# Two heads' attention scores of the prompt as one product with 128 stationary columns

## The chip, the cores and the metric

The kernel runs on one core of a Trainium2 chip. Its engines work from queues of their own: TensorE (PE in the rows, with its weight loads as PEld), VectorE (DVE), ScalarE (ACT), GpSimd (POOL) and SyncE (SP, which here issues the transfers). The metric is the device time of one launch in microseconds (us), as the median of the runs; lower is better. Before the change it is 1457.76 us.

## The reference

Two layers of a streaming encoder run over 512 prompt frames and 8 running streams of 16 frames, model width 1024. Each layer does

    hn   = rms_norm(x);  proj = hn @ w_in            # u_a, g_a, u_b, q, k, v
    out_a = RG-LRU(u_a, g_a)                          # conv, gates, linear scan
    out_b = S5(u_b)                                   # complex state space scan
    out_c = attention(rope(q), rope(k), v)            # 8 query heads, 2 kv heads, 64 wide
    x = x + concat(out_a, out_b, out_c) @ w_out
    x = x + square(relu(rms_norm(x) @ w_up)) @ w_down

and a last norm follows. The change is in the prompt's attention. Frames are in chunks of 64; a chunk's queries see their own chunk's keys and those of the two chunks before (64 keys for the first chunk, 128 for the second, 192 from then on). Four query heads share one kv head, and a learned sink enters each softmax:

    scores = einsum('bnqkgd,bnskd->bnkgqs', qc, kb) * 64 ** -0.5
    probs  = sink_softmax(scores, sinks, mask)
    out    = einsum('bnkgqs,bnskd->bnqkgd', probs, vb)

## The kernel before

All frames are in two groups g of 320 columns: 256 prompt frames and 64 frames of four streams. Activations stand with the features on the 128 partitions. A weight product (`product`, lines L252 to L254) makes a tile of 128 by 320 from 24 matmuls: the weights are split into a high part `wh` (ScalarE, L243) and a low part `wl` (VectorE, L244), each made for four of the eight blocks of 128 rows at a time. So every 12 matmuls need one `wh` and one `wl`, and a late `wl` holds TensorE up in the row L254.

The program writes, for a layer, the input projection of a group (`in_proj`), then the group's mixers (`lru`, `s5`, `attention`), and then output projections and MLP. The order on each engine is not the written one: a list scheduler with a time model of its own places every instruction when the program is built, so products fill TensorE while the mixers' short steps go through VectorE, ScalarE and GpSimd. Whatever changes an instruction's modelled time can move all that follow. Each engine then runs its queue strictly in the order placed.

`attention` works through chunks cq = 0 to 3 and both kv heads. `probs` (L869 to L879) makes the scores of four heads in a PSUM bank: two pairs pr of two heads s each, on the partitions 64 s to 64 s + 63. Query head tile i = 2 pr + s holds kv head 0 on the partitions 0 to 63 and kv head 1 on 64 to 127, so one matmul (L878) contracts over 64 partitions, has 64 stationary columns (a chunk's queries of one head) and streams nk = 64, 128 or 192 keys. In fp32 each written matmul is two records in the trace; per call of `probs` there are 8, and 32 calls in the program. Then `soft` takes the maximum (L818), the offset (L822), the exponentials (ACT, L824) with sums, and scales (L828 to L833). `turned` (transposes L176, copies L890 and L892) and `values` (L899, outputs L903 and L904) follow. Scores, transposes and values share the two PSUM banks `att`. The streams' own attention has its scores in L839, copies in L849 and its values in L857.

Other names that matter: S5's output matmuls L753 and L755, which wait for VectorE's L744; S5's input products L721, which contract over 64 partitions with 128 stationary columns; L269 splits the normalised activations of the next product, L689 and L783 the mixers' outputs; L739 and L680 are scans; L663 the RG-LRU gate products. The rotated queries are written by L609 in `in_evac`.

Of the kernel before, what the change touches and what calls it, by code (L numbers as in the profile page):

```python
# [11 lines left out]
F32 = mybir.dt.float32  # L12
# [38 lines left out]
def _cols(a):  # L51
    """(..., 128 r) vectors as columns."""
    a = np.asarray(a)
    return a.reshape(-1, 128).T
# [5 lines left out]
def _layout(inputs):  # L60
    """The arrays in the order in which the chip reads them: moves of elements only."""
# [6 lines left out]
    def tiles(w):  # L68
        # (1024, 128 n) -> (n, 128 p, 8 k, 128)
        return w.reshape(8, 128, -1, 128).transpose(2, 1, 0, 3)  # L70
# [9 lines left out]
    # small vectors, one column each  # L80
# [13 lines left out]
    # S5 input and output matrices: halves (re, im) and (im, re) on the partitions  # L94
# [53 lines left out]
def encoder_kernel(ctx: ExitStack, tc: tile.TileContext, a, o):  # L148
# [35 lines left out]
    # ------------------------------------------------------------ constants  # L184
# [4 lines left out]
    # the table of the exponentials comes in before the first load has landed  # L189
# [41 lines left out]
    # ------------------------------------------------------------ weights  # L231
# [25 lines left out]
    # ------------------------------------------------------------ norms  # L257
    class Norm:
# [41 lines left out]
        def rsqrt(self):  # L300
            """8/3 / sqrt(mean + eps) with the tokens on the partitions (0-127, 128-255, 192-319)."""
            x = self.bank[:, 320:323]
            w = tp.tile([128, 2, 3], F32, tag="rsq", name="rsq", bufs=2)
            wi = tp.tile([128, 3], I32, tag="rsqi", name="rsqi", bufs=2)
            t, y = (w[:, i] for i in range(2))
            y0 = wi.bitcast(F32)
            # a first guess from the exponent, one step of second order and one of third
            V.tensor_scalar(wi, x.bitcast(I32), -0.5, 1597463007.0, OP.mult, OP.add)
            V.scalar_tensor_tensor(t, y0, -0.5, y0, OP.mult, OP.mult)
            tt(t, t, x, OP.mult)  # L310
            V.scalar_tensor_tensor(y, t, 1.5, y0, OP.add, OP.mult)
            V.scalar_tensor_tensor(t, y, -1.0, y, OP.mult, OP.mult)
            tt(t, t, x, OP.mult)
            V.scalar_tensor_tensor(y0, t, 10.0 / 3, t, OP.add, OP.mult)
            V.scalar_tensor_tensor(y, y0, 5.0, y, OP.add, OP.mult)
            return y
# [14 lines left out]
    # ------------------------------------------------------------ small vectors  # L331
# [6 lines left out]
    # ------------------------------------------------------------ accurate exp on small tiles  # L338
    def exp_small(out, x, n):
        """out = exp(x) on [128, n], to about one unit in the last place."""  # L340
        w = stile(128, 4, n)
        k, f, p, e = (w[:, i] for i in range(4))
        ki = stile(128, n).bitcast(I32)
        V.tensor_scalar(k, x, 1.4426950408889634, 12582912.0, OP.mult, OP.add)
        V.tensor_scalar(k, k, 12582912.0, None, OP.subtract)
        V.tensor_scalar(k, k, -126.0, 126.0, OP.max, OP.min)
        V.scalar_tensor_tensor(f, k, -0.693359375, x, OP.mult, OP.add)
        V.scalar_tensor_tensor(f, k, 2.12194440054690583e-4, f, OP.mult, OP.add)
        V.tensor_scalar(p, f, 1.0 / 5040, 1.0 / 720, OP.mult, OP.add)
        for c in (1.0 / 120, 1.0 / 24, 1.0 / 6, 0.5, 1.0, 1.0):  # L350
            tt(p, p, f, OP.mult)
            V.tensor_scalar(p, p, c, None, OP.add)
        V.tensor_scalar(e, k, 127.0, 8388608.0, OP.add, OP.mult)
        V.tensor_copy(ki, e)
        tt(out, p, ki.bitcast(F32), OP.mult)

    # ------------------------------------------------------------ LRU constants
# [24 lines left out]
    # ------------------------------------------------------------ S5 constants  # L382
# [49 lines left out]
    def cmul(eng, out, jout, wr, wis, z, jz, tmp, conj=False):  # L432
        """out = w z (stacked halves), jout = its halves swapped; wis has the half's sign."""
# [9 lines left out]
    def s5_const(L):  # L443
# [10 lines left out]
        # input matrices: slot s of a pair of groups is abar^(3-s) Bbar  # L454
# [15 lines left out]
        # output matrices  # L470
# [9 lines left out]
        # causal products inside a block: those with the block's last output, then the rows moved up  # L480
# [9 lines left out]
        # rotation tables by doubling  # L490
# [37 lines left out]
    # ------------------------------------------------------------ per layer small tensors  # L528
# [12 lines left out]
    # ------------------------------------------------------------ input projection  # L541
    def gelu2(eng, out, x):
        """out = 2 gelu(x)"""
        w = tp.tile([128, NG], F32, tag="gw", name="gw", bufs=1)
        eng.tensor_tensor(w, x, x, OP.mult)
        eng.tensor_scalar(w, w, 0.044715, 1.0, OP.mult, OP.add)
        eng.tensor_tensor(w, w, x, OP.mult)
        act(w, w, AF.Tanh, scale=0.7978845608028654)
        V.scalar_tensor_tensor(out, w, 1.0, x, OP.add, OP.mult)
# [4 lines left out]
    def in_alloc():  # L554
# [3 lines left out]
        q.q = tp.tile([128, 4, 256], F32, tag="q", name="q", bufs=2)  # L558
# [6 lines left out]
    def in_evac(L, P, g, q, kind, i, pt):  # L565
# [34 lines left out]
        else:  # L600
# [5 lines left out]
            if kind == "q":  # L606
                t = tp.tile([128, NG], F32, tag="t", name="t", bufs=2)
                tt(t, pt, q.cosr, OP.mult)
                tt(q.q[:, i], t[:, 0:256], sw[:, 0:256], OP.add)  # L609
# [31 lines left out]
    # ------------------------------------------------------------ RG-LRU  # L641
    def lru(L, P, g, q, mix, c):
# [10 lines left out]
        for ct in range(2):  # L653
# [4 lines left out]
            # the newest rows before the convolution  # L658
# [7 lines left out]
            # decay a = exp(-2 w) and 1 - a^2 = tanh(w) (1 + a)^2  # L666
# [7 lines left out]
        # injection of the running states into the column before each sample  # L674
# [18 lines left out]
    # ------------------------------------------------------------ S5  # L693
    def s5(L, P, g, q, mix, c):
        K = P["S5"]
        u = q.ub
        # zz takes the place of U
# [5 lines left out]
        # inputs by blocks: rows (group of the pair, t, channel)  # L703
# [41 lines left out]
        # outputs  # L745
# [18 lines left out]
        # states after the last block  # L764
# [22 lines left out]
    # ------------------------------------------------------------ attention  # L787
    def attention(L, P, g, q, mix, c):
        # the samples' scratch
        kcT, p = c.at(0, 2, 2, 144), [c.at(640 + 288 * n, 2, 144) for n in range(2)]  # L790
        vc, pt = c.at(1280, 2, 2, 128), [c.at(640 + 288 * n, 2, 128) for n in range(2)]
        # those of the second pair of samples start at partition 32
        half = [slice(32 * n, 32 * n + 16) for n in range(2)]
        vn, pn = ([c.at(o, 2, 128)[h] for h in half] for o in (1792, 2048))
        # the prompt's, in the same place: keys' windows of 192 columns with 64 zeros on each side
# [18 lines left out]
        def soft(b, x, sk, nsk, one):  # L814
            """Exponentials of the scores in b over their sum with the sink's."""
# [53 lines left out]
        def probs(cq, kv):  # L869
            j, kts, nk, k0, st, w0 = geo(cq)  # L870
            pe, ps, q0 = pes[kv], slice(64 * kv, 64 * kv + 64), 64 * cq
# [4 lines left out]
            for pr in range(2):  # L876
                for s in range(2):
                    mm(b[64 * s:64 * s + 64, pr, 0:nk], lhsT=q.q[ps, 2 * pr + s, q0:q0 + 64], rhs=kT[ps, k0:k0 + nk], start=True, stop=True)  # L878
# [53 lines left out]
    # ------------------------------------------------------------ output projection and MLP  # L932
# [39 lines left out]
    # ------------------------------------------------------------ the program  # L972
# [14 lines left out]
    # the tensor engine's clock rises while the first loads are under way  # L987
# [31 lines left out]
    # ------------------------------------------------------------ final norm  # L1019
# [36 lines left out]
```

## Time and profile before

| | |
|---|---|
| median of 3 runs | 1457.76 us (1455.7 to 1457.97) |
| the profiled execution (its span, first to last instruction) | 1454.2 us |
| what the median has beside the span | 3.6 us |
| TensorE busy | 1404.7 us, 97% |
| VectorE busy | 924.5 us, 64% |
| ScalarE, GpSimd busy | 662.4 us, 377.0 us |
| mean granted TensorE clock | 0.979 |

Time lost shows in three ways: as idle time of the engine that sets the pace, as busy time that a different shape would shorten, and as stretches in which the granted TensorE clock is 0.50. The profile's busy time of TensorE counts pipelined matmuls with modelled ends, so how long a block of matmuls takes is read from its start to the start of what follows.

### The profile page before, as it was taken

The numbers are of one execution on the slowest core, as the hardware profiler recorded it, in microseconds if no ns is written. First come the engines' busy times: TensorE is split into PE (matmuls) and PEld (weight loads), VectorE is DVE, ScalarE is ACT, GpSimd is POOL, SyncE is SP. The second block draws the span as 40 slices with busy tenths as digits, with TensorE's granted clock in tenths as the row PEclk, the third lists the DMA queues.
The fourth block names the chain that finished last, engine by engine and source line by source line (L and its number), as shares of the span: only waits on it lengthen the run. The fifth ranks groups of instructions, "written<-read, shape, count | busy, mean of one in ns | idle before, by whom it ended". The sixth has DMA issues, their size and how long they took to land.

```text
span 1454.2 us, 25829 instructions
## 1 busy us (share of the span) xinstructions
PE 1404.7 (97%) x9540; PEld 1336.3 (92%) x9540; DVE 924.5 (64%) x1858; ACT 662.4 (46%) x1387; POOL 377.0 (26%) x565
## 2 busy tenths in 40 slices
PE   7699999999999999999999999999999999999997
PEld 7688688899999999999987898789999999999997
DVE  8999889856544344357687768875664434434564
ACT  6566565545422122135674667453543312313543
POOL 3847269401010011072244225320110100100111
PEclk9999899999999999999998999899999999999998
DMA  6232122344422222234422342224443222223452
GB/s 244 86 109 81 50 95 97 105 150 140 152 80 78 76 80 73 73 107 157 140 91 73 120 137 92 68 95 145 149 146 106 73 73 73 80 78 104 153 174 94
DMA packets 91389, 156.27 MB, mean 107 GB/s; under 512 B 14336, under 2 KB 18304, under 8 KB 91264
## 3 DMA queue, kind: packets, MB, share of 16 engines
q1 hardware_dynamic: 91264, 154.63, 32.0%
q8 instruction: 75, 1.23, 0.4%
q14 instruction: 50, 0.41, 0.1%
HBM read 151.02 MB, written 3.37 MB: 106 GB/s over the span
## 4 chain that ended last, share of the span: by engine, by line
PE 80%; DVE 11%; POOL 4%; issue 3%; ACT 2%; DMA 1%; SPq 0%; DVEq 0%; POOLq 0%
PE mm L254 24%; PE mm L252 24%; PE mm L253 24%; DVE wl L244 2%; PE att L899 1%; PE att L878 1%; PE s L755 1%; PE s L753 1%; PE att L176 1%; PE s L176 1%; PE fin L326 0%; PE att L663 0%; PE s L721 0%; PE s L779 0%; DVE bigr L269 0%
## 5 line engine op out<-in xcount | busy, mean ns | idle before, releaser
L254 PE MATMUL mm<-bigr,wl 128*128 128x320 f32 x2688 | 840.9, 314 | 22.6 <-DVE wl L244 22.6
L252 PE MATMUL mm<-bigr,wh 128*128 128x320 f32 x2688 | 840.2, 313 | 1.7 <-ACT wh L243 1.1
L253 PE MATMUL mm<-bigr,wh 128*128 128x320 f32 x2688 | 839.1, 313 | 1.0 <-DVE bigr L269 1.0
L243 ACT ACTIVATE wh<-raw 128x512 fp32r<-128x512 f32 x544 | 340.7, 630 | 494.4 <-PE mm L253 469.9
L254 PEld LDWEIGHTS mm<-bigr,wl 128*128 128x128 f32 x2688 | 509.8, 190 | 34.7 <-DVE wl L244 27.4
L252 PEld LDWEIGHTS mm<-bigr,wh 128*128 128x128 f32 x2688 | 509.4, 190 | 7.9 <-issue 5.0
L253 PEld LDWEIGHTS mm<-bigr,wh 128*128 128x128 f32 x2688 | 509.5, 190 | 6.9 <-issue 3.9
L244 DVE TENSOR_TENSOR wl<-raw,wh 128x512 fp32r<-128x512 f32 x544 | 399.7, 736 | 179.6 <-ACT wh L243 158.9
L156 POOL TENSOR_SCALAR bigr<-t 128x320 fp32r<-128x320 f32 x128 | 63.0, 493 | 566.3 <-ACT t L952 566.3
L934 DVE TENSOR_TENSOR xT<-xT,mm 128x320 f32<-128x320 f32 x160 | 77.7, 486 | 127.5 <-PE mm L254 127.4
L952 ACT ACTIVATE t<-t 128x320 f32<-128x320 f32 x128 | 59.9, 470 | 137.9 <-DVE t L951 132.3
L954 DVE TENSOR_TENSOR bigr<-t,bigr 128x320 fp32r<-128x320 f32 x128 | 69.7, 546 | 69.6 <-POOL bigr L156 69.3
L951 DVE SCALAR_TENSOR_TENSOR t<-mm,r 128x320 f32<-128x320 f32 x124 | 60.6, 488 | 81.5 <-PE mm L254 81.4
L288 POOL TENSOR_TENSOR ss<-ss,sq 128x320 f32<-128x320 f32 x58 | 56.9, 981 | 195.7 <-ACT sq L281 185.6
L833 POOL TENSOR_SCALAR att<-att,st 128x192 f32<-128x192 f32 (+3 forms) x40 | 37.2, 931 | 79.5 <-DVE st L831 43.6
L824 ACT ACTIVATE att<-att,st 128x192 f32<-128x192 f32 (+3 forms) x80 | 30.7, 389 | 28.3 <-DVE st L822 22.1
L269 DVE SCALAR_TENSOR_TENSOR bigr<-xT,sm,bigr 128x320 fp32r<-128x320 f32 x64 | 39.7, 629 | 3.8 <-ACT bigr L268 3.6
L268 ACT ACTIVATE bigr<-xT,sm 128x320 fp32r<-128x320 f32 x64 | 34.4, 558 | 11.1 <-DVE xT L934 7.8
L281 ACT ACTIVATE sq<-xT 128x320 f32<-128x320 f32 x66 | 30.4, 460 | 9.9 <-DVE xT L934 3.7
L878 PE MATMUL att<-kT,q 64*64 64x192 f32 (+2 forms) x256 | 28.1, 329 | 2.5 <-ACT att L824 2.1
L605 POOL TENSOR_TENSOR sw<-sw,cs 128x320 f32<-128x320 f32 x20 | 19.4, 969 | 33.6 <-ACT sw L604 28.3
L176 PE MATMUL att<-ident,att 128*128 128x128 f32 (+1 forms) x144 | 24.6, 280 | 3.2 <-DVE att L833 1.0
(287 smaller groups left out, 1078.6 us busy)
## 6 DMA issues: line engine op xcount, KB each, us to landing
raw<-w_up SPq DMA_DIRECT2D x192, 256.0 KB, 2.6
raw<-w_down SPq DMA_DIRECT2D x192, 256.0 KB, 2.6
raw<-w_in SPq DMA_DIRECT2D x96, 256.0 KB, 2.6
raw<-w_out SPq DMA_DIRECT2D x64, 256.0 KB, 2.5
xT<-x SPq DMA_DIRECT2D x8, 320.0 KB, 5.7
yT<-xT SPq DMA_DIRECT2D x8, 320.0 KB, 2.5
cs<-rope SPq DMA_DIRECT2D x4, 320.0 KB, 4.4
gg<-gg SPq DMA_DIRECT2D x2, 512.0 KB, 5.1
```

Of the source, the lines that this page charges most:

```text
L156: return G.tensor_scalar(out, in_, 1.0, 0.0, OP.mult, OP.add)
L176: PE.transpose(out, in_, ident[0:n, 0:n])
L243: act(h, raw, AF.Copy)
L244: tt(l, raw, h.bitcast(F32), OP.subtract)
L252: mm(pt, lhsT=h[:, k % 4], rhs=m[:, k, 0], start=k == 0, stop=False)
L253: mm(pt, lhsT=h[:, k % 4], rhs=m[:, k, 1], start=False, stop=False)
L254: mm(pt, lhsT=l[:, k % 4], rhs=m[:, k, 0], start=False, stop=k == 7)
L288: G.tensor_tensor(self.ss, self.ss, sq, OP.add)
L934: tt(xT[:, g, k], xT[:, g, k], pt, OP.add)
L951: V.scalar_tensor_tensor(t, pt, 0.0, norm.r, OP.max, OP.mult)
L952: act(t, t, AF.Square)
L954: tt(am[:, f, 1], t, am[:, f, 0].bitcast(F32), OP.subtract)
```

## The change

The queries' tile gets the order head pair partition, chunk, head, query (`[128, 4, 4, 64]`, as the streams' tile `qS` has it), so that a chunk's queries of two heads lie in one run of 128 columns. L609 writes it with four runs of 64 elements. `probs` makes a pair's scores in one matmul with 128 stationary columns, in place of two with 64 columns each on the two halves of the PSUM partitions. Operands, key columns, sums and the PSUM tile are otherwise the same. The diff without removed comments:

```
-        q.q = tp.tile([128, 4, 256], F32, tag="q", name="q", bufs=2)
+        q.q = tp.tile([128, 4, 4, 64], F32, tag="q", name="q", bufs=2)
...
-                tt(q.q[:, i], t[:, 0:256], sw[:, 0:256], OP.add)
+                c4 = lambda z: z[:, 0:256].rearrange("p (c q) -> p c q", q=64)
+                tt(q.q[:, :, i], c4(t), c4(sw), OP.add)
...
-            pe, ps, q0 = pes[kv], slice(64 * kv, 64 * kv + 64), 64 * cq
+            pe, ps = pes[kv], slice(64 * kv, 64 * kv + 64)
...
             for pr in range(2):
-                for s in range(2):
-                    mm(b[64 * s:64 * s + 64, pr, 0:nk], lhsT=q.q[ps, 2 * pr + s, q0:q0 + 64], rhs=kT[ps, k0:k0 + nk], start=True, stop=True)
+                mm(b[:, pr, 0:nk], lhsT=q.q[ps, cq, 2 * pr:2 * pr + 2].rearrange("p i q -> p (i q)"), rhs=kT[ps, k0:k0 + nk], start=True, stop=True)
```

The lines from L609 to L877 of the kernel before are one further down in the one after, and L878 stays L878. The scheduler places the instructions anew. Up to the first L878 the order is the same; it differs from there to about 300 us of the trace before, and in small moves in the second layer between 750 and 970 us. Two places follow.

TensorE's queue in the first layer, group 0, ahead of S5's first output matmuls (L755 before, L756 after). Before:

```order
L252 MATMUL mm<-bigr,wh 128x320
L755 MATMUL s_1154<-Cm,bigf 80x64
...
L755 MATMUL s_1155<-Cm,bigf 80x64
L878 MATMUL att<-kT,q 64x192 x4
L899 MATMUL att<-att,vt 64x256 x2
```

After:

```order
L254 MATMUL mm<-bigr,wl 128x320
L878 MATMUL att<-kT,q 128x192 x2
L899 MATMUL att<-att,vt 64x256 x2
L252 MATMUL mm<-bigr,wh 128x320
...
L756 MATMUL s_1154<-Cm,bigf 80x64
L756 MATMUL s_1155<-Cm,bigf 80x64
```

The scores of a chunk and the values of the chunk before it have moved from behind S5's output matmuls to six product matmuls ahead of them.

VectorE's queue in the first layer, group 1, around two successive low parts `wl` of the output projection's weights. In the kernel before (the two `wl` are the third and the fifth row):

```order
L830 TENSOR_TENSOR st_2300<-st_2300 128x2
L680 SCALAR_TENSOR_TENSOR bigf<-bigf,coll 128x332 x2
L244 TENSOR_TENSOR wl<-raw,wh 128x512
L830 TENSOR_TENSOR st_2315<-st_2315 128x2
L244 TENSOR_TENSOR wl<-raw,wh 128x512
```

In the kernel after (L745, L850, L819 and L690 are L744, L849, L818 and L689 of before; the two `wl` are the second and the last row):

```order
L745 TENSOR_TENSOR bigf<-bigf 128x640
L244 TENSOR_TENSOR wl<-raw,wh 128x512
L850 COPY att<-att 16x256
L819 TENSOR_REDUCE st_2321<-att 128x2
L690 SCALAR_TENSOR_TENSOR bigr<-bigf,bigr 128x2x320
L269 SCALAR_TENSOR_TENSOR bigr<-xT,sm,bigr 128x320 x2
L745 TENSOR_TENSOR bigf<-bigf 128x640
L269 SCALAR_TENSOR_TENSOR bigr<-xT,sm,bigr 128x320
L244 TENSOR_TENSOR wl<-raw,wh 128x512
```

Between the two `wl` stands one short step before, and seven steps, most of them long, after; the scans L680 and the streams' softmax steps have moved ahead of both.

## Rows read from the trace of the kernel before

**Rows 1.** The page: busy time, share of the span and instructions of TensorE.

```profile
PE 1404.7 (97%) x9540; PEld 1336.3 (92%) x9540; DVE 924.5 (64%) x1858; ACT 662.4 (46%) x1387; POOL 377.0 (26%) x565
```

**Rows 2.** Windows: stretch, its length, busy time by engine, granted clock, DMA.

```profile
99.00:152.00 53.00, 47.82 (x334) 42.13 (x332) 52.51 (x124) 33.66 (x88) 36.07 (x44) 0.89 0.28 87
150.85:161.05 10.20, 9.72 (x51) 7.42 (x52) 8.25 (x23) 4.88 (x17) 3.00 (x8) 0.50 0.32 105
161.10:200.00 38.90, 38.57 (x262) 29.61 (x261) 27.87 (x58) 25.43 (x58) 12.01 (x15) 1.00 0.15 50
200.00:220.00 20.00, 16.68 (x108) 15.49 (x106) 20.00 (x27) 10.78 (x27) 16.28 (x17) 0.83 0.30 95
220.00:260.00 40.00, 39.33 (x275) 32.98 (x275) 39.09 (x75) 20.50 (x54) 38.91 (x53) 0.96 0.29 94
1000.00:1400.00 400.00, 400.00 (x2732) 399.62 (x2732) 199.93 (x358) 140.48 (x246) 35.20 (x64) 1.00 0.32 108
```

**Rows 3.** Timeline of TensorE: score blocks of 192, 128, 64 keys, and what follows.

```profile
141.86 0.87 PE L878 MATMUL att<-kT,q 64*64 64x192 f32 x8
142.66 0.41 PE L254 MATMUL mm<-bigr,wl 128*128 128x320 f32 x1
...
119.56 0.65 PE L878 MATMUL att<-kT,q 64*64 64x128 f32 x8
120.15 0.41 PE L254 MATMUL mm<-bigr,wl 128*128 128x320 f32 x1
...
99.23 0.45 PE L878 MATMUL att<-kT,q 64*64 64x64 f32 x8
99.61 0.63 PE L253 MATMUL mm<-bigr,wh 128*128 128x320 f32 x1
```

**Rows 4.** Timeline of TensorE: matmuls with 128 stationary columns, and what follows.

```profile
180.16 0.82 PE L663 MATMUL att<-bigf,gg 128*128 128x332 f32 x2
180.92 1.12 PE L721 MATMUL s<-bigf,Bm 64*128 64x80 f32 x8
181.96 0.41 PE L252 MATMUL mm<-bigr,wh 128*128 128x320 f32 x1
```

**Rows 5.** Groups of VectorE by shape: busy us, mean ns of one.

```profile
L609 DVE TENSOR_TENSOR q<-t,sw 128x256 f32<-128x256 f32 x16 | 7.4, 465 | 0.0
```

**Rows 6.** Timeline of TensorE around S5's first output matmuls.

```profile
151.33 0.80 PE L755 MATMUL s<-Cm,bigf 128*80 128x64 f32 x4 [1.48 <-DVE bigf L744]
...
155.62 1.55 PE L878 MATMUL att<-kT,q 64*64 64x192 f32 x8
157.09 1.12 PE L899 MATMUL att<-att,vt 128*64 128x256 f32 x4
158.14 0.64 PE L253 MATMUL mm<-bigr,wh 128*128 128x320 f32 x1
```

**Rows 7.** Timeline of TensorE: the longest wait of group 1.

```profile
206.55 0.64 PE L254 MATMUL mm<-bigr,wl 128*128 128x320 f32 x1 [2.81 <-DVE wl L244]
```

**Rows 8.** Timeline of VectorE, steps that the change puts between two `wl`.

```profile
214.75 0.68 DVE L244 TENSOR_TENSOR wl<-raw,wh 128x512 fp32r<-128x512 f32 x1
...
215.75 1.69 DVE L744 TENSOR_TENSOR bigf<-bigf 128x640 f32<-128x640 f32 x1
...
224.44 1.49 DVE L689 SCALAR_TENSOR_TENSOR bigr<-bigf,bigr 128x640 fp32r<-128x640 f32 x1
225.86 0.55 DVE L818 TENSOR_REDUCE st<-att 128x2 f32<-128x384 f32 x1
...
227.10 1.10 DVE L269 SCALAR_TENSOR_TENSOR bigr<-xT,sm,bigr 128x320 fp32r<-128x320 f32 x2
...
228.62 0.99 DVE L269 SCALAR_TENSOR_TENSOR bigr<-xT,sm,bigr 128x320 fp32r<-128x320 f32 x1
```

**Rows 9.** Timeline of TensorE: S5's output matmuls of group 1, and what follows.

```profile
212.31 0.44 PE L755 MATMUL s<-Cm,bigf 128*80 128x64 f32 x4
...
214.70 0.39 PE L253 MATMUL mm<-bigr,wh 128*128 128x320 f32 x1
```

## Prediction

> **What bounds the kernel now.** I read the page's first part, then windows, then the timelines of TensorE and VectorE around the score matmuls. TensorE is busy for 97% of the span [rows 1], and from 1000 to 1400 us it is busy all the time: 400 us for 2732 matmuls, 0.146 us for a product matmul [rows 2]. There TensorE's work is the time. In the first layer's mixers it is not so throughout. From 99 to 152 us VectorE is busy for 52.51 of 53.00 us, TensorE for 47.82; from 200 to 220 us VectorE for all 20.00, TensorE for 16.68; from 220 to 260 both nearly always (39.09 and 39.33 of 40) [rows 2]. Between, from 161 to 200 us, TensorE is the one that never rests: 38.57 of 38.90 us. So a TensorE edit counts in full in the MLP and in the stretches between, and little where VectorE sets the pace; there the order of VectorE's queue counts. One more thing costs time: from 150.85 to 161.05 us the granted clock is 0.50, which is 1.2 of 2.4 GHz [rows 2]; what stands ahead of its fall is told with term 2.
>
> **The score matmuls themselves.** The names say that half of the matmuls go. What they cost is read from a block's start to the start of what follows: 0.80 us with 192 keys (141.86 to 142.66), 0.59 with 128 (119.56 to 120.15), 0.38 with 64 (99.23 to 99.61) [rows 3]. Each block has 8 records. From 128 to 192 keys it grows by 0.21 us, 3.3 ns a key; one record takes 0.83 ns a key, as L663 shows: two records of 332 columns in 0.76 us with the fixed parts [rows 4], of which 2 x 332 x 0.83 are 0.55. So the block grows as four records do, not as eight: eight in a row would need 8 x 0.16 = 1.28 us alone, and the block has 0.80. The two heads' matmuls, on the two column halves, already run side by side. The new block has four records of as many keys, in four slots: nothing is won from the halved count.
>
> What it adds is the weight load. 128 stationary columns from 64 partitions are what L721 has: eight records of 80 columns take 1.04 us (180.92 to 181.96) [rows 4]. Streaming would be 8 x 80 x 0.83 ns = 0.53; so the load sets the step. With the last record's streaming (0.07) and the 0.09 that the fixed end takes, 0.88 are left for eight loads, 0.11 each. The block of 192 keys has 0.80 - 4 x 0.16 = 0.16 of fixed parts: the same 0.09 and 0.05 to 0.07 for the first load of 64 columns. So the load takes 0.11 with 128 columns and half of that with 64, and it hides under a record that streams longer. New blocks:
> - 192 keys: 0.11 + 4 x 0.16 + 0.09 = 0.84 to 0.85, against 0.80: 0.05 more, for the first load;
> - 128 keys: 4 x 0.11 + 0.11 + 0.09 = 0.64 against 0.59: 0.05 more;
> - 64 keys: load-bound, 4 x 0.11 + 0.05 + 0.09 = 0.58 against 0.38: 0.20 more.
>
> Of 32 blocks, 24 have 192 keys, 4 have 128 and 4 have 64. Five (two, two and one) lie before 152 us, where VectorE covers them; they cost 0.6 if that cover is gone. The rest are 23 x 0.05 + 2 x 0.05 + 2 x 0.20 = 1.65; one of the short ones of the second layer runs at the lower clock, where it costs twice as much. **Term 1: +1.8 us**; bounds 0 (every first load hidden behind the matmul ahead) and +2.4 (no cover).
>
> The Trainium skill has a rule that goes further against the change: "TensorE: Matmul & The Clock Gate", "Part 3: Packing small matmuls", lets a weight load overlap a running matmul only when their row groups differ. By that rule the new records, all on one row group, would each pay their load. The rows differ: L663's two records use all rows, and 0.76 us hold one load (0.11), 0.55 and 0.09, not two loads. What the rule would give as a mechanism of this kernel is the fourth rival.
>
> **The write of the queries.** L609 takes 465 ns as one run of 256 [rows 5]; it becomes four runs of 64. The 16 of them lie in the input projections beside product matmuls. I take 0; bounds from a tenth less to a tenth more, 16 x 0.05 = 0.7 either way, only if VectorE is last there.
>
> **The moved order, group 0 of the first layer.** Before, TensorE comes to S5's output matmuls at 151.33 after a wait of 1.48 us for L744, and the lower clock sets in there; scores and values of a chunk come after them, 155.62 to 158.14 us, 2.52 us at the lower clock [rows 6]. In the new order these two stand ahead. Their softmax steps have moved up on VectorE too, so I expect them to be ready. They take 0.85 + 1.05 = 1.9 us at the higher clock and so fill the wait. VectorE's L744 itself gets later by what is now ahead of it, a copy of 256 columns (put at the 0.47 of L609's 256 [rows 5]) and two steps of two columns (put at 0.2 each): about 0.9. So 2.52 leave the path and 0.9 come in. **Term 2: -1.6 us**; bounds -2.5 (no delay) and +0.9 (scores not ready, delay in full). In 99 to 152 us the set of VectorE's steps is otherwise the same up to a few places, and it is the bound: 0.
>
> **The moved order, group 1 of the first layer.** Two low parts that follow each other with a step of 0.15 between now have 1.69 (L744), 1.49 (L689), 0.55 (L818), 1.10 and 0.99 (three L269) between them [rows 8], 5.8 us, and the second itself takes 0.7. TensorE has in this time, counted from L744's end: S5's output matmuls, 212.31 to 214.70, 2.4 us [rows 9], transposes 0.4, eleven product matmuls 1.6: 4.4 us. The first low part takes 0.7 of VectorE in front. So the second comes 0.7 + 5.8 + 0.7 = 7.2 us after L744, and TensorE stands for 2.8 us. Against that, the streams' transposes, a score block and the scans have been done ahead, while TensorE waited for `wl` anyway: the trace has 2.81 us of such a wait [rows 7]. I set 1.4 of it against the new wait: half of the old wait filled. **Term 3: +1.4 us**; bounds -2.8 (all of the old wait gone and no new one) and +2.8.
>
> In the second layer the blocks move by a few matmuls, with VectorE's queue nearly as before; SP's queue moves some small transfers by a few places. I take 0 for both.
>
> **The sum.** 1454.2 of the profiled span + 3.6 that the median has beside it = 1457.8; + 1.8 - 1.6 + 1.4 = **1459.4 us**, 0.1% above the median. About 0.2% (2.9 us) is what a measurement of this kernel can tell from no change.
>
> **Rivals.**
> 1. *The clock stays up.* With the wait ahead of S5's output matmuls filled, the stretch 150.85 to 161.05 is granted 2.4 GHz. It then has 5.1 us to give; VectorE is busy in it for 8.25 of 10.20 us, which leaves some 2 to 4. For it: the fall stands right behind the wait. Against: the new order has a short wait there still (0.9 less the fill). With term 3 at 0: 1459.4 - 4 - 1.4 = 1454.0. This is the way to a faster kernel.
> 2. *The new wait of group 1 is paid in full and lowers the clock.* The place is the second `wl` behind L744, L689 and L269. The price is 2.8 for the wait, and as before behind the wait of 2.81, a stretch at the lower clock: 20 us at 0.83 [rows 2] are 3.4 lost. 1457.8 + 1.8 - 1.6 + 2.8 + 3.4 = 1464.2. It decides from the point where TensorE's waits between 203 and 222 us sum to over 5 us, against 3.3 (16.68 busy of 20) before.
> 3. *The change does what its name says:* the heads' matmuls ran one after another, and half goes: 24 blocks x 4 x 0.16 + 4 x 4 x 0.11 + 4 x 4 x 0.05 = 18 us, 1440. The blocks' lengths speak against it.
> 4. *No load overlaps in the new block* (the rule above): three more loads of 0.11 in each of 32 blocks, 10.6 us, 1470. L663 speaks against it.
>
> **How the numbers follow.** Forecast 0.43, its own range 1456 to 1462; rival 1 0.25; rival 2 0.27; rival 3 0.02; rival 4 0.03. The order is most of the uncertainty, since a scheduler that places everything anew can win or lose a wait of 3 us, and the clock doubles what a wait costs. Range 1452 to 1465: it takes in rivals 1 and 2 and leaves out 3 and 4 and the tails. Faster: rivals 1 and 3, 0.27. Slower: rivals 2 and 4, 0.30. Within 0.2%: 0.43.
>
> **What would show it.** L878 with 128 records of form 64*128; a block of 192 keys 0.84 to 0.85 us long up to what follows, of 64 keys near 0.58. If 0.80 stands, term 1 is wrong; if near 0.45, the pairs never overlapped; if over 1.1, loads are paid each. For term 2: L878 and L899 ahead of the first L755, and no wait over 1 us at it. For term 3: a wait of 2 to 3 us at a low-part row L254 after S5's output matmuls of group 1. The forecast as a whole is wrong if the stretch 99 to 300 us changes by over 3 us either way, or if the second layer does.

## The result and the profile after

The changed kernel takes 1464.93 us (median of 4 runs, 1463.28 to 1466.50) against 1457.26 for the kernel before on the same chip: a ratio of 1.0055, with a 95% interval of 1.0041 to 1.0069. On a second chip (below) it was 1.0041, from 1.0024 to 1.0057. So it is slower by 0.4 to 0.55%, 6 to 8 us; the forecast of 1459.4 us, no change, was wrong, although the time lies in the range given.

The page of the kernel after, its first part (answering to [rows 1]) and the group of score matmuls from its fifth part (line, engine, operation, tiles, shape, count | busy us, mean ns of one | idle before):

```profile
PE 1414.7 (97%) x9412; PEld 1347.0 (92%) x9412; DVE 925.5 (63%) x1858; ACT 664.5 (45%) x1387; POOL 380.7 (26%) x565
...
L878 PE MATMUL att<-kT,q 64*128 64x192 f32 (+2 forms) x128 | 28.8, 348 | 0.3 <-ACT att L825 0.2
```

The same group in the kernel before:

```profile
L878 PE MATMUL att<-kT,q 64*64 64x192 f32 (+2 forms) x256 | 28.1, 329 | 2.5 <-ACT att L824 2.1 <-DVE st L830 0.4
```

128 records have gone, as the name of the change says, and TensorE is busy for 10.0 us longer. The score group itself takes no less with half the records: 28.8 us against 28.1. The other engines are busy about as long as before.

Windows of the kernel after (stretch, length, busy time of TensorE, its weight loads, VectorE, ScalarE, GpSimd, granted clock, DMA share, GB/s), the first four answering to rows of [rows 2]:

```profile
99.00:152.00 53.00, 48.04 (x311) 41.85 (x310) 51.06 (x123) 33.28 (x89) 34.29 (x43) 0.93 0.26 81
200.00:220.00 20.00, 17.60 (x124) 15.43 (x123) 20.00 (x28) 11.29 (x24) 17.95 (x14) 1.00 0.29 96
220.00:260.00 40.00, 37.67 (x236) 31.43 (x235) 36.06 (x71) 19.63 (x56) 39.88 (x53) 0.87 0.27 88
1000.00:1400.00 400.00, 400.00 (x2733) 399.81 (x2732) 197.26 (x347) 139.61 (x243) 32.54 (x60) 1.00 0.32 107
...
164.60:174.80 10.20, 9.93 (x36) 6.25 (x35) 6.14 (x20) 3.30 (x14) 1.88 (x2) 0.50 0.00 0
226.00:236.20 10.20, 10.20 (x55) 8.34 (x52) 7.55 (x15) 3.85 (x12) 10.20 (x17) 0.50 0.18 61
```

The MLP is as it was (400 us, 2733 matmuls). The stretch at 0.50 that began behind the wait of 1.48 us [rows 6] has shrunk from 10.20 to 3.4 us, but two new ones of 10.20 us stand at 164.60 and 226.00, where TensorE hardly waits at all: 9.93 and 10.20 us busy. Summed over the span, the two profiles have 60.9 us at 0.50 before and 74.8 after (the 63 and 77 of the expectations below take in some 2 us behind the span's end), while TensorE's waits of over 0.15 us come to 42.4 and 42.5.

TensorE's timeline after (start, length, engine, line, operation, tiles, shape, count, in brackets the wait ahead and what ended it). Blocks of 64, 128 and 192 keys answer to [rows 3], the waits to [rows 6, 7, 9]:

```profile
113.32 0.66 PE L878 MATMUL att<-kT,q 64*128 64x64 f32 x4
113.90 0.42 PE L254 MATMUL mm<-bigr,wl 128*128 128x320 f32 x1
...
122.44 0.71 PE L878 MATMUL att<-kT,q 64*128 64x128 f32 x4
123.08 0.42 PE L254 MATMUL mm<-bigr,wl 128*128 128x320 f32 x1
...
149.49 0.41 PE L254 MATMUL mm<-bigr,wl 128*128 128x320 f32 x1 [2.41 <-DVE wl L244]
149.83 0.92 PE L878 MATMUL att<-kT,q 64*128 64x192 f32 x4
151.21 1.12 PE L899 MATMUL att<-att,vt 128*64 128x256 f32 x4 [0.46 <-DVE att L892]
...
154.02 0.57 PE L756 MATMUL s<-Cm,bigf 128*80 128x64 f32 x4
...
162.17 0.92 PE L878 MATMUL att<-kT,q 64*128 64x192 f32 x4
163.02 0.33 PE L176 MATMUL att<-ident,att 128*128 128x128 f32 x1
...
210.25 0.41 PE L254 MATMUL mm<-bigr,wl 128*128 128x320 f32 x1 [0.58 <-DVE wl L244]
...
215.71 0.50 PE L756 MATMUL s<-Cm,bigf 128*80 128x64 f32 x4 [1.17 <-DVE bigf L745]
...
220.99 0.42 PE L254 MATMUL mm<-bigr,wl 128*128 128x320 f32 x1 [0.57 <-DVE wl L244]
...
773.88 0.41 PE L254 MATMUL mm<-bigr,wl 128*128 128x320 f32 x1 [1.54 <-DVE wl L244]
...
776.58 0.79 PE L756 MATMUL s<-Cm,bigf 128*80 128x64 f32 x4 [1.41 <-DVE bigf L745]
```

In the second layer the kernel before has one wait there, not two:

```profile
769.64 0.50 PE L755 MATMUL s<-Cm,bigf 128*80 128x64 f32 x4 [1.74 <-DVE bigf L744]
```

Where it went, counted by the product matmuls (L252 to L254), which both kernels issue in the same number: the start of the 1250th, near 330 us, is 5.7 us later after than before and stays so until 624 us; the 5000th, near 990 us, is 10.5 us later and stays so to the end. So these two profiles lose 5.7 us in the first layer's mixers, 4.8 around the second's, and nothing elsewhere.

Within the first layer the count of product matmuls alone misleads, because the new order has moved other matmuls past them. At the starts of the 580th, the 640th and the 1040th both kernels have done the same number of each kind of matmul, so there the times can be compared. The 580th (behind S5's first output matmuls, group 0) starts 2.1 us earlier after than before, the 640th 4.5 us later, the 1040th 5.7 us later. The loss is thus made between the 580th and the 640th. Windows of this work, before:

```profile
159.65:195.55 35.90, 35.57 (x238) 26.61 (x237) 24.59 (x57) 22.21 (x57) 9.41 (x11) 0.98 0.13 41
```

And after:

```profile
157.52:200.06 42.54, 41.71 (x231) 31.36 (x229) 30.42 (x70) 27.30 (x70) 13.41 (x21) 0.84 0.16 50
```

It takes 6.6 us more, with TensorE's waits of over 0.15 us at 0.2 us before and 0.6 after; 1.4 us of it before and 13.7 after stand at 0.50, so the lower clock takes some 6.1 of the 6.6 us. In this stretch TensorE goes through a long run of small matmuls (S5, gates, transposes, scores, values) without a product matmul. In the kernel before, the run lies between these two rows:

```profile
161.47 0.31 PE L254 MATMUL mm<-bigr,wl 128*128 128x320 f32 x1
...
176.89 0.54 PE L252 MATMUL mm<-bigr,wh 128*128 128x320 f32 x2
```

In the kernel after, between these:

```profile
158.70 0.31 PE L254 MATMUL mm<-bigr,wl 128*128 128x320 f32 x1
...
183.79 0.57 PE L252 MATMUL mm<-bigr,wh 128*128 128x320 f32 x2
```

The run lasts 15.4 us before, all at the higher clock, and 25.1 us after, 10.2 of them at 0.50: the new order has put 22 more small records into it (104 before; 118 after, which are 126 when a product counts as the pair of before).

**How the runs are read.** The clock differs from one execution of a kernel to the next, so one profile is one draw: 29 runs of the kernel before on one chip (the first block of the table) spread from 1453.15 to 1466.98 us, the three shortest at mean granted clocks of 0.976 to 0.978, the three longest at 0.969 to 0.970. Every run lists its span and its mean granted clock. Span times clock is the time that would be left if TensorE had the higher clock throughout and was the bound (below: "at full clock"); the rest of the span is what the lower clock took (below: "clock"). Means over all runs of a kernel, in us, with the standard error of the first part; each block of the table is one chip with its own runs of the kernel before. The ratio, with its interval, is what the verdicts use; medians of kernels whose runs spread this much can differ by more (form alone: 3.0 us, a ratio of 1.0004):

| kernel | median | ratio, 95% interval | at full clock | clock |
|---|---|---|---|---|
| before (29 runs) | 1456.21 | | 1420.4 ± 0.5 | 35.1 |
| new form, old order | 1459.20 | 1.0004 (0.9982 to 1.0025) | 1422.9 ± 0.7 | 33.9 |
| old form, new order | 1464.90 | 1.0049 (1.0027 to 1.0072) | 1421.8 ± 0.8 | 41.0 |
| new form, new order in layer 1 only | 1462.38 | 1.0033 (1.0014 to 1.0051) | 1423.0 ± 1.0 | 37.1 |
| before (23 runs) | 1457.07 | | 1421.4 ± 0.4 | 34.6 |
| after, again | 1463.51 | 1.0041 (1.0024 to 1.0057) | 1425.4 ± 0.7 | 36.6 |
| after, waits filled | 1456.41 | 0.9989 (0.9975 to 1.0003) | 1431.9 ± 0.7 | 22.9 |
| before, waits filled | 1449.47 | 0.9935 (0.9911 to 0.9959) | 1430.3 ± 1.5 | 17.4 |
| before (23 runs) | 1458.11 | | 1421.0 ± 0.5 | 35.9 |
| new form, old order, waits filled | 1448.14 | 0.9931 (0.9908 to 0.9954) | 1432.1 ± 1.9 | 14.2 |
| after, filled, 24 spares more | 1459.31 | 0.9999 (0.9978 to 1.0019) | 1436.5 ± 1.0 | 21.0 |
| after, filled, 48 spares more | 1458.70 | 1.0011 (0.9997 to 1.0025) | 1442.5 ± 0.7 | 15.1 |
| before, filled, 19 spares more | 1449.07 | 0.9940 (0.9919 to 0.9962) | 1433.5 ± 0.4 | 14.2 |
| before (17 runs) | 1459.12 | | 1420.3 ± 0.6 | 36.6 |
| low parts first | 1455.29 | 0.9976 (0.9963 to 0.9989) | 1423.2 ± 0.6 | 30.2 |
| new form, filled, low parts first | 1450.44 | 0.9945 (0.9924 to 0.9966) | 1429.1 ± 0.5 | 20.3 |

The split is rough: 0.001 of clock, its last digit, is 1.5 us. The Trainium skill ("TensorE: Matmul & The Clock Gate", "Terms") prices a clock that passes K of N pulses in the same way, at its time by 1 - K/N. The 29 runs of one kernel agree in sign and less than fully in size: their spans fall by 1.1 us for each 0.001 of clock.

### The profile page after: what moved, and what is told of

It reads as the page before. It is cut to its first block, busy times and chain, and to the rows that moved or that the text cites. A ratio compares the mean times of both kernels' runs of the same rounds, so it can differ in the third digit from the quotient of the medians.

```text
span 1464.7 us, 25563 instructions
## 1 busy us (share of the span) xinstructions
PE 1414.7 (97%) x9412; PEld 1347.0 (92%) x9412; DVE 925.5 (63%) x1858; ACT 664.5 (45%) x1387; POOL 380.7 (26%) x565
## 4 chain that ended last, share of the span: by engine, by line
PE 80%; DVE 11%; POOL 3%; issue 3%; ACT 3%; DMA 0%; SPq 0%; DVEq 0%; POOLq 0%
PE mm L252 24%; PE mm L253 24%; PE mm L254 24%; DVE wl L244 2%; PE att L899 1%; PE att L878 1%; PE s L756 1%; PE s L754 1%; PE att L176 1%; PE s L780 1%; DVE bigr L269 1%; PE fin L326 1%; ACT wh L243 1%; PE att L858 0%; PE s L176 0%
## 5 line engine op out<-in xcount | busy, mean ns | idle before, releaser
L254 PE MATMUL mm<-bigr,wl 128*128 128x320 f32 x2688 | 840.3, 313 | 24.0 <-DVE wl L244 23.9
L252 PE MATMUL mm<-bigr,wh 128*128 128x320 f32 x2688 | 841.9, 314 | 1.2 <-ACT wh L243 1.1
L254 PEld LDWEIGHTS mm<-bigr,wl 128*128 128x128 f32 x2688 | 509.8, 190 | 33.6 <-DVE wl L244 29.1
L252 PEld LDWEIGHTS mm<-bigr,wh 128*128 128x128 f32 x2688 | 509.7, 190 | 9.6 <-issue 6.1
L834 POOL TENSOR_SCALAR att<-att,st 128x192 f32<-128x192 f32 (+3 forms) x40 | 39.4, 985 | 83.1 <-DVE st L832 47.2
L878 PE MATMUL att<-kT,q 64*128 64x192 f32 (+2 forms) x128 | 28.8, 348 | 0.3 <-ACT att L825 0.2
```

The lines of the kernel that those rows point to most:

```text
L252: mm(pt, lhsT=h[:, k % 4], rhs=m[:, k, 0], start=k == 0, stop=False)
L254: mm(pt, lhsT=l[:, k % 4], rhs=m[:, k, 0], start=False, stop=k == 7)
```

## The experiments

**Form and order apart.** The diff changes two things: the matmul, and through the scheduler the place of many instructions on every engine. The order was therefore fixed from outside. Each engine's list of one kernel was written down and put on the other as issue order without waits; a pair of 64-column matmuls takes the place of its one product and the other way round. The added code, shortened:

```diff
+    for e, listed in _ORDER.items():        # per engine
+        last = None
+        for n in listed:
+            for i in units[e][n]:           # one instruction, or a pair of products
+                if last is not None:
+                    tc.add_manual_dep(i, last.name, issue_order_only)
+                last = i
```

The new form in the old order:

> The one product with 128 stationary columns, with every engine's instructions kept in the order of the kernel before (a pair's place is taken by its product). Theory A (the moved order costs the time, mostly by stretches at a granted clock of 0.50): only the longer blocks remain, 2.0 us, so 1459.3 us (1457.5 to 1461), and TensorE stands at 0.50 for about as long as before, 63 us. Theory B (the form itself lowers the clock or costs, whatever the order): 1463 to 1465, with some 77 us at 0.50. Theory C (the two together): near 1461.

Measured: 1.0004, with 2.5 us more at full clock (1422.9 against 1420.4; term 1 has 2.0 with its cover gone) and by the means over all runs no more time at the lower clock than before (33.9 against 35.1). Its one profile has 74.2 us at 0.50, about theory B's figure, but its 12 runs have a mean granted clock of 0.977 against 0.976 for the 29 runs of the kernel before, so this profile is a draw to the low side. The median lies in theory A's range. The form alone can't be told from no change; the interval leaves room for 3.6 us.

The old form in the new order:

> The two products with 64 stationary columns and the old layout of the queries, with every engine's instructions in the order of the changed kernel. Theory A: 1464.9 less the 2.0 us of the longer blocks, so 1463 us (1461.5 to 1465), with some 77 us at the granted clock of 0.50. Theory B: as before, 1457.3 (1456 to 1459), with some 63 us at 0.50. Theory C: near 1461.

Measured: 1.0049, nearly the changed kernel's own loss without its matmul. 5.9 us of it lie in the clock and 1.4 at full clock; its profile has 87.3 us at 0.50. Theory A holds, theory B falls.

The new form with the new order in the first layer's part of every list and the old order in the rest:

> The one product throughout, the order of the changed kernel in the first layer and that of the kernel before in the second. Between before and after the first layer's mixers took 5.7 us more and the second's 4.6. Theory A: both by the order, so the second layer gives its 4.6 us back but for the 1 us of its blocks: 1461.3 us (1460 to 1462.5). Theory B: no difference to the changed kernel, 1464.9. A third theory D, that the second layer's loss comes from the form and the first's from the order, gives 1464.9 here and 1461.5 to 1462 for the product in the old order.

Measured: 1.0033, within theory A's bounds and between the form alone (1.0004) and the changed kernel (1.0041 to 1.0055). Most of the loss is the first layer's order; for the second's 0.001 to 0.002 is left, which these intervals don't separate from nothing. The profiles don't put it down to the order either: from the 3700th to the 5000th product matmul, around the second layer's mixers, this kernel takes 296.6 us and the form alone, with the same instructions in the same order there, 292.6 (after: 297.5 and, once more, 296.5; before: 292.9; old form, new order: 292.5). Windows of the profile before and of the old form in the new order, over the first layer's mixers. Before:

```profile
90.00:300.00 210.00, 198.25 (x1342) 167.88 (x1342) 183.17 (x389) 120.04 (x311) 124.22 (x164) 0.93 0.28 88
```

The old form in the new order:

```profile
90.00:300.00 210.00, 198.63 (x1299) 167.40 (x1299) 178.81 (x383) 117.70 (x307) 129.23 (x164) 0.89 0.26 82
```

TensorE is busy equally long in the first layer's mixers, but gets through 43 records fewer in the same 210 us: the clock stands at 0.89, not at 0.93.

**The changed kernel once more,** beside the filled kernels on one chip:

> The changed kernel once more, beside the two below on one chip. By the runs of its two halves (the product in the old order, ratio 1.0004; the old products in the new order, 1.0049) the sum is 1.0053, so some 1463 to 1465 where the kernel before has 1456 to 1457, with the mean granted clock lower by 0.002 to 0.004.

Measured: 1.0041. Of the 6 us, 4.0 are at full clock (the blocks and some 1.5 to 2 us of waits) and 2.0 in the clock. The mean clock is lower by 0.0012 (0.9750 against 0.9762), less than the 0.002 to 0.004 expected. Its profile has 68.0 us at 0.50, where the first one had 74.8: the first trace alone overstates the clock's share.

**Is it the clock, and do the waits bring it down?** Spare products that nobody reads were put on TensorE ahead of the instructions at which it waited:

```diff
+    def fill(n):
+        for m in n:
+            z = bank("fin")
+            for _ in range(m):
+                mm(z[:, 0:128], lhsT=ident, rhs=ident, start=True, stop=True)
```

> The changed kernel in its own order, with 57 spare products of the identity with itself (128 columns, 0.213 us each, 12 us in all; their results are read by nobody) put on TensorE just ahead of the instructions at which it waited over 0.4 us between 95 and 270 us and between 740 and 1000 us. Theory W (the clock falls in or after TensorE's waits): with the waits filled the stretches at 0.50 shrink from some 65 us in the mixers to 35 or less, which gives back 10 to 15 us: 1450 to 1455. Theory T (it falls because the small products of the attention and of S5 keep the array little busy, waits or not): the stretches stay, and the spare products cost what they overlap, 0 to 4 us: 1464 to 1469.

> The kernel before in its own order, with 62 of the same spare products ahead of its waits of over 0.4 us in the same stretches. Theory W: the stretches at 0.50 in the mixers shrink from some 51 us to 25 or less, 1442 to 1449. Theory T: 1457 to 1461.

Measured (58 spares after, one more than the expectation counts, and 62 before): by the medians each gains some 7 us (7.1 and 7.6), and the kernel before with its waits filled is faster than either kernel, 0.9935. TensorE works 6.5 and 8.9 us more at full clock and gets 13.7 and 17.2 back from the clock. That filling the waits brings the clock back is shown, and in both orders alike, so the waits are not what sets the two kernels apart. Whether it is idle time as such that lets the clock fall, or too little work in the stretch around it, these two runs don't separate: spare products between matmuls bring it back too (below), at a higher price. The sizes that theory W gave were somewhat too large: 1456.4 against 1450 to 1455, and 1449.5 against 1442 to 1449. TensorE's timeline of the filled changed kernel, at the wait of 2.41 us:

```profile
147.97 2.40 PE L793 MATMUL fin<-ident 128*128 128x128 f32 x20
150.56 0.41 PE L254 MATMUL mm<-bigr,wl 128*128 128x320 f32 x1 [0.19 <-DVE wl L244]
```

Ten spare products stand where the wait was, and they don't hold up the low part: VectorE runs some 1.05 us later than in the profile without spares, by the same amount ahead of the spares as behind them. The longest stretches that the filled changed kernel keeps at 0.50 in the mixers:

```profile
165.30:175.50 10.20, 10.04 (x37) 6.65 (x38) 5.75 (x20) 3.37 (x14) 1.87 (x2) 0.50 0.00 0
230.20:237.00 6.80, 6.80 (x27) 6.00 (x27) 5.69 (x12) 3.35 (x9) 6.80 (x11) 0.50 0.16 55
786.60:796.80 10.20, 10.20 (x42) 8.76 (x40) 3.70 (x12) 2.76 (x10) 1.29 (x2) 0.50 0.08 25
```

The work from the 580th to the 640th product matmul, in the filled kernel before:

```profile
156.08:191.32 35.24, 34.91 (x238) 25.95 (x236) 26.34 (x64) 23.84 (x61) 12.19 (x17) 1.00 0.17 53
```

And in the filled changed kernel:

```profile
157.20:199.71 42.51, 40.68 (x233) 30.43 (x231) 30.15 (x69) 26.39 (x66) 13.09 (x20) 0.88 0.16 48
```

So 7 us still lie between the two kernels by the medians. Between these two profiles, 9.0 us apart, 7.3 us are lost in this one stretch, 5.1 of them to the 10.2 us at 0.50 and 1.5 to waits (1.7 us against 0.2).

**Is this rest the order too?**

> The one product in the order of the kernel before, with the 62 spare products of that order ahead of its waits. With the waits filled the two orders still lay 7 us apart (1456.4 and 1449.5). Theory O (the order makes that gap, through stretches at 0.50 that hold no product of the projections): only the form's longer blocks are added to the filled kernel before, 1451.5 us (1450 to 1453). Theory F (with the waits gone the form makes it): 1455 to 1457.

Measured: 1448.14, below theory O's range of 1450 to 1453, so the form costs nothing that shows. The clearest pair of the study is this kernel and the filled changed kernel (on two chips, whose kernels before agree within 1.3 us): the same matmuls, about as many spares, 1432.1 and 1431.9 us at full clock, and 14.2 against 22.9 us for the clock. The work from the 580th to the 640th product matmul, in the new form and the old order, against the 42.51 us above in the new order:

```profile
156.81:191.80 34.99, 34.66 (x230) 26.01 (x228) 26.25 (x63) 23.76 (x61) 12.13 (x17) 1.00 0.17 55
```

One profile is one draw, but all that were taken agree on this stretch. The seven kernels in the old order (four of them with spares) take 35.0 to 36.4 us for it, with 0 to 3.2 us at 0.50, and none of it begins there: it is the end of an earlier stretch. The seven profiles in the new order (the changed kernel twice) take 39.4 to 47.7 us, and six of them have 6.8 to 17.1 us at 0.50; the seventh is the kernel with two spares at a place, next.

**Does more work between the small products hold the clock there?** Single or double spares between the small products of the stretches left at 0.50 (24 places, where the expectation counts 25):

> The filled changed kernel with 25 more spare products (5.3 us at full clock), one every 1.2 us or more between the small products of the four stretches that stood at 0.50 (160 to 175, 222 to 235, 774 to 789, 919 to 931 us of the changed kernel). Theory T2 (once the waits are filled, it is the lack of work between small products that lets the clock fall there): the 37 us at 0.50 in the mixers shrink to 20 or less, which gives 8 us back against some 3 to 5 us of the spare products: 1450 to 1454. If more small work does not hold the clock: 1458 to 1463.

> The same with two spare products at each of those places (10.5 us). Theory T2: the clock holds, but the spare products now cost about what it gives: 1453 to 1458. If it does not hold the clock: 1462 to 1468.

> The filled kernel before with 19 more single spare products between the small products of its stretches at 0.50 (214 to 224, 771 to 785, 914 to 934 us). Theory T2: up to 17 us at 0.50 are left in the mixers to win from, 8 us at most, against 2 to 4 us of spare products: 1445 to 1450, so a version as fast as the filled one or faster. If small work does not hold the clock: 1452 to 1455.

Measured: 1459.31, 1458.70 and 1449.07; the first lies where single spares don't hold the clock, the second between the two ranges, the third in theory T2's range. One spare at each place adds 4.6 us at full clock and gives back 1.9; two add 10.6 and give back 7.8. The second layer's mixers do stand at 1.00 with one spare, yet the first layer keeps a stretch of 17.10 us at 0.50 that is busy from end to end:

```profile
162.20:179.30 17.10, 17.10 (x65) 12.29 (x64) 7.14 (x24) 3.87 (x15) 1.53 (x3) 0.50 0.04 15
```

With two spares at each place the clock does hold there. The work from the 580th to the 640th product matmul in its profile:

```profile
159.44:200.31 40.87, 40.22 (x268) 31.91 (x266) 27.85 (x65) 26.43 (x66) 12.23 (x19) 1.00 0.13 40
```

So theory T2 is borne out for the clock, as far as one profile shows it, and falls as a way to gain time: of a spare product inside a wait a third to a half is paid for by the wait (62 of 0.213 us, 13.2 us, cost 8.9; 58 cost 6.5), one between matmuls is paid nearly in full. In the kernel before the 19 more cost 3.2 us at full clock and give back 3.2.

**The waits taken away instead of filled.** Four low parts ahead of TensorE's long waits were issued earlier on VectorE; all else stands in the old order. Two of the four moves:

```diff
 L818 TENSOR_REDUCE st<-att 128x2
+L244 TENSOR_TENSOR wl<-raw,wh 128x512
 L739 SCALAR_TENSOR_TENSOR bigf<-tab,bigf 128x640
+L244 TENSOR_TENSOR wl<-raw,wh 128x512
 L820 TENSOR_SCALAR st<-st,nsks 128x2
...
-L244 TENSOR_TENSOR wl<-raw,wh 128x512
 L820 TENSOR_SCALAR st<-st,nsks 128x2
-L244 TENSOR_TENSOR wl<-raw,wh 128x512
```

> The kernel before (two products of 64 columns, no spare products), its order changed in four places of VectorE's queue alone: the low parts (wl) that TensorE waited for at 206.55, 657.54 and 913.01 us are issued ahead of steps that nobody waited for, 1.3 to 4.4 us earlier (two ahead of the scan and of its two-column step at 200.07 and 202.47, one ahead of L954 at 654.29, one ahead of L742 at 910.94). If these waits cost both their own length and the clock behind them (theory W): 5 us of waits go, and some 17 us at 0.50 that stood right behind the waits at 205.5 and 912.0 shrink to half: 1448 to 1452. If VectorE only turns up late elsewhere: 1455 to 1459.

> The one product of 128 columns in the order of the kernel before with the same four low parts earlier, and 43 spare products ahead of the waits that are left (the two places of 12 and 13 cut to 3). Theory W: the filled kernel in the old order (1448.1) less some 3 to 5 us of waits that had been filled but not taken away: 1443 to 1446. If the low parts' move only shifts VectorE's lateness: 1447 to 1451.

Measured: 0.9976, a gain of 3.5 us, but not the 5 to 9 expected (the median, 1455.29, lies in the range for a VectorE that turns up late elsewhere): 6.4 us less for the clock, 2.9 more at full clock. With spares it is 0.9945 (1450.44, again in the range for the move that only shifts the lateness), no better than the spares alone. TensorE's timeline of the first of the two:

```profile
205.00 0.39 PE L252 MATMUL mm<-bigr,wh 128*128 128x320 f32 x1 [1.71 <-DVE xT L934]
...
215.57 0.64 PE L254 MATMUL mm<-bigr,wl 128*128 128x320 f32 x1 [3.71 <-DVE wl L244]
...
912.84 0.63 PE L254 MATMUL mm<-bigr,wl 128*128 128x320 f32 x1 [2.69 <-DVE wl L244]
```

The wait of 2.81 us at 206.55 [rows 7] is gone; one of 1.71 us stands at 205.00 (0.50 before) and one of 3.71 us nine us later, for the next low part; that at 913 us is hardly shorter (2.69 us, 2.99 before). VectorE is the bound in these stretches, and what is taken forward there pushes something else back.

## Why the prediction was wrong, step by step

- **Term 1, the blocks, was right.** 113.32 to 113.90, 122.44 to 123.08 and 162.17 to 163.02 are 0.58, 0.64 and 0.85 us, as worked out, and the form alone has 2.5 ± 0.8 us more at full clock (2.0 worked out without cover). Nothing was won from the halved count. The rule of the Trainium skill ("TensorE: Matmul & The Clock Gate", "Part 3: Packing small matmuls") that loads on one row group don't overlap fails here: the block has no 0.33 us more, and its form alone is at 1.0004, not at the 1470 us of rival 4.
- **Term 2, group 0: its sum came out in its own place, by another wait.** As the prediction put it, L878 and L899 stand ahead of the first L756, which waits no more. But TensorE waits 2.41 us for a low part just ahead of them. The term charged VectorE's additional steps to L744 alone; they stand ahead of that low part as well, and so does a write of the streams' queries (L612) that takes 1.56 us here, where L611 took 0.21 in the kernel before. VectorE's timeline after:

```profile
145.44 0.81 DVE L743 TENSOR_TENSOR bigf<-bigf,tab 128x640 f32<-128x640 f32 x1
146.18 0.16 DVE L829 TENSOR_TENSOR st<-sm,st 128x2 f32<-128x2 f32 x1
146.26 0.41 DVE L610 TENSOR_TENSOR q<-t,sw 128x256 f32<-128x256 f32 x1
146.59 1.56 DVE L612 TENSOR_TENSOR qS<-t,sw 128x64 f32<-128x64 f32 x1
148.07 1.36 DVE L244 TENSOR_TENSOR wl<-raw,wh 128x512 fp32r<-128x512 f32 x1
```

Even so the 580th product matmul, behind this place, starts 2.1 us earlier after than before (1.6 in the second profile of the changed kernel), where the term has -1.6. That the number fits is in part luck.
- **The step that failed is what the prediction gave the stretch behind: nothing.** It read 161 to 200 us as the stretch in which TensorE never rests, at a granted clock of 1.00 [rows 2], and let the new order change nothing there. The work from the 580th to the 640th product matmul takes 35.9 us before and 42.5 and 39.4 us in the two profiles of the changed kernel, 6.6 and 3.5 us more, with TensorE's waits at 0.6 and 0.5 us; 13.7 and 6.8 us of it stand at 0.50. The order's sum, -1.6 + 1.4 + 0, was made of waits, place by place, and has no term for this. Measured over all runs, the order is the changed kernel against the form alone, 0.0037 (5.4 us), or the order alone against the kernel before, 0.0049 (7.1 us), with intervals of some 3 to 4 us either way. By these two pairs 1.5 and 1.4 us of it stand at full clock (waits); the larger part, 3.1 and 5.9 us, is time at the lower clock.
- **Term 3, group 1: right in sum, wrong in its steps.** From the 640th to the 1040th product matmul the two profiles of the changed kernel lose 1.2 and 1.0 us, near the +1.4, but no wait of 2 to 3 us came at a low part behind S5's output matmuls; there are 0.58, 1.17 and 0.57 us. The steps between the two low parts, priced at 5.8 us from rows in which some of them ran long [rows 8], and without the copy L850, took 3.65 us (216.61 to 220.26), L745 (L744 before) for one 0.81 in place of 1.69. VectorE's timeline after:

```profile
216.61 0.40 DVE L850 COPY att<-att 16x256 f32<-16x256 f32 x1
...
219.06 0.81 DVE L745 TENSOR_TENSOR bigf<-bigf 128x640 f32<-128x640 f32 x1
...
220.26 0.67 DVE L244 TENSOR_TENSOR wl<-raw,wh 128x512 fp32r<-128x512 f32 x1
```

So the sum is near by luck.
- **The second layer was set to 0** because its blocks move by a few matmuls. The first profile lost 4.8 us there, with two waits (1.54 and 1.41 us) in place of one of 1.74; by the runs it is 0.001 to 0.002 of the span, and the profiles of one order there differ by as much (296.6 and 292.6 us).
- **Rival 2 gave the right size, 1464.2 us, by the wrong place and cause.** It was to decide where waits between 203 and 222 us sum to over 5 us; from 200 to 220 they sum to 2.4 (17.60 busy of 20). Time at the lower clock did come, but in group 0 and in a stretch without such a wait, and filling the waits left it there. Rival 1 went the other way: the stretch at 150.85 shrank as it said, and others grew.
- **The queries' write at 0** stands: L610 takes 0.41 us as four runs of 64, where L609 took 0.465 [rows 5].

**What stays open.** In the new order TensorE has 22 more small records in a row than in the old one (15.4 us of them before, 25.1 after), and the clock falls within that run. Whether the length of the run brings it down, or which small matmuls it holds, or what stands ahead of it, was not separated; no run puts product matmuls back into it. Two spares at a place held the clock there, single ones did not, each by one profile. That group 0 has the larger part of the first layer's loss is read from profiles; no run has the new order in one group alone.

The fastest versions keep the old order, in either form, and have spare products in TensorE's waits: 0.9931 to 0.9945, with intervals that overlap. They beat both kernels.

## What to carry to other kernels

Where a scheduler places everything anew, an edit is two edits: its own cost, which a few block lengths of the trace give to 0.05 us, and a new order, whose cost no local row gave here. Fix the order, measure the form by itself, and keep the old order if it is better. Compare two orders only at points at which both have done the same work, and look at the granted clock in between. Where TensorE waits for 1 to 3 us at a time and the granted clock falls behind it, unread products inside these waits can be worth more than the edit.

## What the runs showed of the hardware that was not expected

- Two matmuls with 64 stationary columns that follow each other on the two column halves cost no more than one with 128: a block of 192 keys takes 0.80 us with two such pairs and 0.85 with two products.
- 62 products of 0.213 us each, 13.2 us of work that nobody reads, make the kernel 0.65% faster: they cost 8.9 us at full clock and return 17.2.
- The clock can stand at 0.50 while TensorE is busy from end to end (17.10 of 17.10 us, 65 records), so a busy share near 100% does not tell that the clock is up.
- Executions of one kernel on one chip spread by 14 us (1453.15 to 1466.98), with the mean clock from 0.978 down to 0.969; a difference of 6 us can't be read from two traces.
